# Dense projections of two mixers: float32 products of 64 stationary columns, in pairs, for three float32r products of split operands

## The chip, the core and the metric

The kernel runs on one core of one Trainium2 chip. The metric is the device time of one execution, in microseconds (us), as the median of three runs. The engines are named as in the profile: PE (TensorE's matmuls), PEld (its weight loads), DVE (VectorE), ACT (ScalarE), POOL (GpSimd), SP (the queue that issues most DMAs). The two operands of a matmul are called stationary (loaded into the array, up to 128 columns of it) and moving (streamed through, here 256 or 512 columns).

## What is computed

Two layers of a decoder trunk on 512 tokens of 1024 features, in float32. Each layer is a mixer and a mixture of experts, with a residual sum and a layer norm after each. Cut to what the change touches:

```python
# layer 0: RWKV-7 (8 heads x 64) and causal pooling (windows 2, 4, 8, 16)
p = x @ w_in                               # 1024 -> 2304 features
y_rwkv = ...                               # delta-rule state, head norm, bonus, gate
y_pool = ...                               # pooled groups times pool_w
y = concatenate([y_rwkv, y_pool]) @ w_out  # 1024 -> 1024
x = layer_norm(ALPHA * x + y); x = layer_norm(ALPHA * x + moe(x))
# layer 1: a convolution module (512 channels, width 31) and retention (8 heads x 64)
p = x @ w_in                               # 1024 -> 3072 features
c = silu(norm(depthwise_conv(glu(p[..., :1024]))))
r = group_norm(retention(q, k, v)) * silu(g)
y = concatenate([c, r]) @ w_out
x = layer_norm(ALPHA * x + y); x = layer_norm(ALPHA * x + moe(x))
```

The products with `w_in` and `w_out` are what is called dense below.

## The kernel before

The four parts run one after the other: mixer 0 (to about 336 us of the profiled span), the mixture of layer 0 (to about 512), mixer 1 (to about 836), the mixture of layer 1.

A mixer is written as streams, Python generators that each emit one line of work: `dense` (the projections), `evacuate` (reads each bank of results out of PSUM), `weights` (prepares weights), in mixer 0 `prep`, `solve`, `side`, `states`, `heads` and `pools`, in mixer 1 `turn`, `join`, `kernels`, `taps`, `conv_norm`, `retention`, `ret_norm`. The class `Flow` puts their steps into one order when the program is built: it keeps an expected time for every engine and tile, gives each instruction an expected cost (`cost`, `clocked`), and always takes the stream, by priority, whose next step can start. The chip then runs every engine's instructions in exactly that order. All of them are issued through one helper, so they share line L57 in the profile and are told apart by tile names.

**A dense product** is one step of `unit`: 128 rows of the contraction times one bank of results. It adds into a PSUM tile `pp` of 128 partitions by 512 or 256 columns. In mixer 0 there are 208 products with 512 moving columns (18 column blocks of `w_in` by 8, and 64 of the output projection). In mixer 1 there are 192 with 256 columns (six jobs `qkv`), 96 with 512 (two `conv` pairs and two `gr` jobs), and 64 with 512 of the output projection. `jobs` lists them in the order of use.

**Precision by splitting.** A float32 operand is kept as two float32r tiles: a rounded copy, made on ACT, and the rest, a subtraction on DVE or POOL. Of weights these are `wh` and `wl` (from the fetched `wr`). x^T lives in four tiles `x` of `x_room`, two high and two low, each for half of the features; what goes into the output projections is split likewise (`yT` and `pT` in mixer 0, `mc` and `mr` in mixer 1). A dense product is then three matmuls of 128 stationary columns: high by high, high by low, low by high. `weights` splits a job's weights two jobs ahead: in mixer 0 the subtraction runs on DVE, in mixer 1 on POOL, but for two halves.

**Mixer 0.** `solve` inverts, for each of four pairs of heads, a triangular matrix by repeated squaring: small products `pi` of 64x64 on PE, an addition into `T` and a transposition `Tt` on DVE, level after level. `dense` steps are put into the gaps.

**Mixer 1.** `taps` does the depthwise convolution on DVE: 4 channel groups by 31 taps, each one instruction `acc<-u,cw,acc` over 128x512. Its input `u` comes from the `conv` jobs. When all taps are done, `conv_norm` normalises over channels, tile by tile, which takes PE transposes of `acc` and back of `cn`; only then can the first half of the output projection run.

After its last reader is gone, the room of x^T is given to other tiles: the stream that loads the first expert weights (`start`) waits for the mark `room`.

Of the kernel before, what the change touches and what calls it, by code (L numbers as in the profile page):

```python
# [14 lines left out]
OP = mybir.AluOpType  # L15
# [15 lines left out]
class Flow:  # L31
    """Puts the work of several streams into one order. A stream is a generator that yields, before each step, the engine
    the step starts on and the tiles it needs; the order follows from when those are expected to be there, with
    `streams` in order of priority."""
# [28 lines left out]
    def cost(e, op, out, ins, alu=None):  # L63
# [91 lines left out]
    def take(self, pool, shape, name, bufs):  # L155
        """a tile of a ring, once the reads of the one before it there have been put in order"""
# [13 lines left out]
    def run(self, streams):  # L170
# [79 lines left out]
class Kernel:  # L250
# [12 lines left out]
    def setup(self):  # L263
# [12 lines left out]
        # x^T of a mixer; after its projections what the mixture of experts starts with  # L276
# [3 lines left out]
    def x_room(self, order=(0, 1, 2, 3)):  # L280
# [10 lines left out]
    def mixer0(self):  # L291
        """Feature-major tiles hold two heads on the partitions and 512 tokens; token-major ones hold two chunks of 64 tokens
        (p = 0, 1) on the partitions, and 4 pairs of chunks, heads and features along them. With L the part of a chunk's
        own tokens, T = (I - L)^-1, W = T a and u0 = T (a k^T v), the state after a chunk is
        decay (S + b^T (W S + u0) + k^T v), so all but the product with S is made for every chunk at once."""
# [6 lines left out]
        with ctx:  # L302
# [19 lines left out]
            # weights in the order of their use  # L322
            # (numbers: columns of the input projection; else rows of the output projection: whose, which, a half of the columns)
# [3 lines left out]
            items = []  # L327
            for job in jobs:
# [5 lines left out]
            raws, halved = {}, {}  # L334
# [7 lines left out]
            def halve(raw, eng, e):  # L342
                """the float32r part of weights, and the rest"""
                hi = wp.tile(list(raw.shape), F32R, name="wh")
                lo = wp.tile(list(raw.shape), F32R, name="wl")
                nk, n = raw.shape[1:]
                cuts = [(slice(0, nk // 2), slice(0, n)), (slice(nk // 2, nk), slice(0, n))] if nk > 1 else [
                    (slice(0, 1), slice(0, n // 2)), (slice(0, 1), slice(n // 2, n))]
                for k, c in cuts:
                    yield "A", (raw,)  # L350
                    A.copy(hi[:, k, c], raw[:, k, c])
                for k, c in cuts:
                    yield e, (hi,)
                    eng.tensor_tensor(lo[:, k, c], raw[:, k, c], hi[:, k, c].bitcast(F32), op=OP.subtract)
                return hi, lo
# [9 lines left out]
            fetch(1)  # L365
            # lnx_g for tokens on partitions
# [22 lines left out]
            for t in range(NT):  # L389
                for g in range(2):  # L390
# [4 lines left out]
                    hi, lo = [xT[j][g][:, :, 128 * t:128 * t + 128] for j in range(2)]  # L395
                    A.copy(hi, ps)
                    V.tensor_tensor(lo, ps, hi.bitcast(F32), op=OP.subtract)
# [6 lines left out]
            yT = [[sp.tile([128, S], F32R, name=f"yT{k}{j}") for k in range(2)] for j in range(2)]  # L404
            yp = sp.tile([128, 4, S], F32, name="yp")
            pT = []
# [5 lines left out]
            def weights():  # L412
                for n in range(len(items)):
                    if n >= 2:
                        yield from wait(("wdone", n - 2))
                    halved[n] = yield from halve(raws.pop(n), V, "V")
                    done.add(("w", n))
                    fetch(n + 2)

            units = []  # L420

            def unit(parts):
                """one bank's worth of products: parts [(left, right)] for every 128 rows"""
# [4 lines left out]
                for k, (lhs, rhs) in enumerate(parts):  # L428
                    yield "PE", (lhs[0], lhs[1], rhs[0], rhs[1])
# [3 lines left out]
                    for i, j in ((0, 0), (0, 1), (1, 0)):  # L433
                        mm(ps, lhs[i], rhs[j], start=k == 0 and i + j == 0, stop=k == len(parts) - 1 and i == 1)
# [5 lines left out]
            def dense():  # L440
                """the input projection and the output projection"""
                for n, job in enumerate(jobs):
                    if not isinstance(job, int):
                        yield from wait(*((job[0], k) for k in job[1]))
                    yield from wait(("w", n))
                    wt = halved.pop(n)
                    if isinstance(job, int):
                        yield from unit([([w[:, k, :] for w in wt], [x[k // 4][:, k % 4, :] for x in xT]) for k in range(KT)])
                        if job == last_in:
                            done.add("x^T")  # L450
                    else:
                        left = pT if job[0] == "p" else yT
                        for t, h in tokens(job[2]):
                            ts = slice(128 * t, 128 * t + 128)
                            c = slice(0, 512) if job[2] is not None else slice(512 * h, 512 * h + 512)
                            yield from unit([([q[:, k, ts] if left is pT else q[k][:, ts] for q in left],
                                              [w[:, i, c] for w in wt]) for i, k in enumerate(job[1])])
                        if job == ("p", (2, 3), 1):
                            done.add("room")
                    done.add(("wdone", n))  # L460
# [1735 lines left out]
```

## Time and profile before

| | us |
|---|---|
| median of three runs | 1039.68 |
| their range | 1038.59 to 1040.19 |
| span of the profiled execution | 1034.8 |
| busy in it: PE | 914.6 |
| DVE | 734.7 |
| ACT | 339.5 |
| POOL | 327.5 |

The profile shows one execution, so the sums below stand against its span; the median of the runs lies 4.9 us above it. The page lists the busy time of each engine over the whole span. For a change in two of four parts that share says little: a view that splits the span at the borders of its stages shows which engine is full in which. Matmuls are pipelined, so the printed duration of one overlaps the next; what a matmul costs is read from start to start.

### The profile page before, as it was taken

To read this page: it belongs to the slowest core of one execution; us is meant where nothing else is said; L and a number is where in the kernel's file an instruction comes from. 1 tells how busy PE (TensorE), PEld (TensorE's weight loads), DVE (VectorE), ACT (ScalarE), POOL (GpSimd) and SP (SyncE) were. 2 spreads that over 40 slices of the span, in tenths; PEclk is the share of its full clock that TensorE was granted. 3 is DMA by queue.
4 is the path that set the end of the run, shared out by engine and by line. 5 is a ranking of instruction groups with operands and counts; after the bars stand their busy time and mean duration, and the time that the engine had idled before them with its cause. 6 is when DMAs were issued, how large, how long until landed. Compare 5 with 4: busy or idle time off the path is not lost. (4 is left out here: it accounts for less than half of the span.)

```text
span 1034.8 us, 18665 instructions
## 1 busy us (share of the span) xinstructions
PE 914.6 (88%) x7364; PEld 644.3 (62%) x7364; DVE 734.7 (71%) x1527; ACT 339.5 (33%) x690; POOL 327.5 (32%) x298
## 2 busy tenths in 40 slices
PE   6999999999995599999879589779999748999993
PEld 5777777777775255545368568778878624545542
DVE  3565868576777977776676999994733698767666
ACT  3543242433214233433353012212502333433333
POOL 2120414135303810100169446663422281100003
PEclk9999999999997799999989789988888969999997
DMA  7210101011176859788152121221325165976742
GB/s 216 82 43 22 43 24 41 24 43 60 43 280 221 307 225 359 274 345 334 42 161 76 47 81 42 82 82 41 116 102 214 62 246 227 347 282 247 306 197 83
DMA packets 60012, 156.97 MB, mean 152 GB/s; under 512 B 5153, under 2 KB 40097, under 8 KB 51728
## 3 DMA queue, kind: packets, MB, share of 16 engines
q1 hardware_dynamic: 54256, 141.79, 37.4%
q0 software_dynamic: 4512, 9.74, 3.0%
q10 hardware_dynamic: 1152, 4.19, 1.0%
q8 instruction: 60, 0.98, 0.4%
q14 instruction: 32, 0.26, 0.1%
HBM read 155.71 MB, written 6.29 MB: 157 GB/s over the span
## 5 line engine op out<-in xcount | busy, mean ns | idle before, releaser
L1874 DVE SCALAR_TENSOR_TENSOR x<-x,pcm 128x512 f32<-128x512 f32 x210 | 137.0, 683 | 54.5 <-PE pcm L1872 54.2
L57 PE MATMUL pp<-x,wh 128*128 128x512 f32 x480 | 163.5, 423 | 6.4 <-DVE u L57 5.1
L57 PE MATMUL pp<-wh,x 128*128 128x256 f32 (+1 forms) x544 | 139.2, 342 | 23.3 <-DVE u L57 11.4
L57 DVE SCALAR_TENSOR_TENSOR acc<-u,cw,acc 128x512 f32<-128x512 f32 x120 | 127.8, 1120 | 0.7
L57 ACT CAST wh<-wr 128x512 fp32r<-128x512 f32 (+1 forms) x82 | 61.8, 776 | 192.5 <-PE pp L57 129.0
L57 PEld LDWEIGHTS pp<-wh,x 128*128 128x128 f32 x544 | 100.2, 209 | 34.6 <-DVE u L57 11.6
L1835 PE MATMUL ph<-we,xt 128*64 128x256 f32 (+1 forms) x928 | 116.8, 389 | 0.0
L57 PEld LDWEIGHTS pp<-x,wh 128*128 128x128 f32 x480 | 85.9, 195 | 29.0 <-issue 6.2
L1872 PE MATMUL pcm<-yh,P 128*128 128x512 f32 x216 | 99.2, 459 | 3.0 <-DVEq L2043 2.3
L57 PE MATMUL pp<-x,wl 128*128 128x512 f32 x240 | 96.3, 401 | 0.0
L57 POOL TENSOR_TENSOR wl<-wr,wh 128x1024 fp32r<-128x1024 f32 x28 | 83.3, 2988 | 34.5 <-ACT wh L57 34.5
L57 PE MATMUL pp<-wl,x 128*128 128x256 f32 (+1 forms) x272 | 91.1, 335 | 0.0
L1872 PE MATMUL pcm<-yl,P 128*128 128x512 f32 x216 | 85.8, 397 | 5.1 <-DVE yl L288 5.1
L1824 ACT ACTIVATE xt<-pt,x 128x128 f32<-128x128 f32 x224 | 84.8, 471 | 15.6 <-PE pt L1818 15.6
L1835 PEld LDWEIGHTS ph<-we,xt 128*64 128x64 f32 (+1 forms) x928 | 56.8, 129 | 47.1 <-issue 31.7
L1738 POOL DMA_INDIRECT xg<-xd,imx x20 | 19.9, 993 | 191.9 <-PE pt L1818 147.3
L1872 PEld LDWEIGHTS pcm<-yh,P 128*128 128x128 f32 x216 | 40.6, 188 | 52.0 <-DVE x L1874 28.7
L57 DVE SCALAR_TENSOR_TENSOR x<-x,pp 128x512 f32<-128x512 f32 x64 | 43.6, 685 | 39.6 <-PE pp L57 39.5
L1857 PE MATMUL py<-we,hT 128*64 128x512 f32 (+1 forms) x232 | 62.8, 628 | 0.4 <-ACT hT L1847 0.4
L288 DVE TENSOR_TENSOR yl<-py,yh 128x512 fp32r<-128x512 f32 x54 | 37.1, 691 | 34.3 <-ACT yh L287 34.3
L1839 ACT ACTIVATE hs<-ph 128x128 f32<-128x128 f32 x28 | 7.8, 277 | 160.0 <-PE ph L1835 160.0
L57 PEld LDWEIGHTS pp<-wl,x 128*128 128x128 f32 x272 | 57.4, 211 | 2.8
(427 smaller groups left out, 1657.7 us busy)
## 6 DMA issues: line engine op xcount, KB each, us to landing
we<-in_c_experts_dram SPq DMA_DIRECT2D x56, 1536.0 KB, 9.5
wr<-in_ev_w_in_dram SPq DMA_DIRECT2D x18, 512.0 KB, 3.9
x<-in_c_experts_dram SPq DMA_DIRECT2D x8, 1024.0 KB, 6.1
wr<-in_od_w_in_dram SPq DMA_DIRECT2D x7, 1024.0 KB, 5.1
wr<-in_ev_w_out_dram SPq DMA_DIRECT2D x8, 512.0 KB, 3.7
x<-in_c_experts_dram SPq DMA_DIRECT2D x8, 512.0 KB, 4.2
xd<-x ACTq DMA_DIRECT2D x8, 512.0 KB, 4.1
wr<-in_od_w_in_dram SPq DMA_DIRECT2D x8, 512.0 KB, 5.7
```

The lines of the kernel that those rows point to most:

```text
L57: r = f(*args, **kw)
L288: (eng or nc.vector).tensor_tensor(lo, src, hi.bitcast(F32), op=OP.subtract)
L1738: G.indirect_dma_start(out=xg[n % NG], out_offset=None, in_=xd, in_offset=bass.IndirectOffsetOnAxis(ap=idx, axis=0), bounds_check=S - 1, o ...
L1824: A.activation(xt[:, kk], ps[:, k], AF.Identity, scale=gc[:, kk:kk + 1], bias=bc[:, kk:kk + 1])
L1835: mm(hp[r], xt[:, k, r], w[0][:, k], start=k == 0, stop=k == KT - 1)
L1839: A.activation(hs, hp[:, 0], AF.Silu)
L1857: mm(ps[r], hT[:, r], w[1][:, h], start=True, stop=True)
L1872: mm(ps, P[:, 128 * t:128 * t + 128], y[:, 512 * half:512 * half + 512], start=n == 0, stop=n == len(ops) - 1)
L1874: V.scalar_tensor_tensor(xs, xs, scale, ps, op0=OP.mult, op1=OP.add, accum_out=total)
```

## The change

Operands are no longer split. Weights go from the fetched tile `wr` straight into the matmuls, x^T is two float32 tiles, and `yT`, `yp`, `acc` and `mr` are single float32 tiles. A dense product becomes a pair of float32 matmuls, one for the first 64 stationary columns, with the results on partitions 0 to 63, and one for the other 64, on partitions 64 to 127 (`paired`). The stream `weights` is gone; `wr` has a ring of five (mixer 0) or four tiles (mixer 1), fetched that far ahead. `Flow.cost` gets an entry for such a matmul, n/2380 us for n columns, so 0.215 us for 512 and 0.43 us for a pair of them. The mark `room` comes at the end of the input projection of either mixer (before: after the pooling half, or the convolution half, of the output projection).

```diff
@@ Flow.cost
                 narrow = ins[0].shape[0] <= 64 and out.shape[0] <= 64
+                if out.shape[0] <= 64 and not narrow:
+                    return max(n / 2380, 0.055)
                 return max(0.027 + n / 1200, 0.08) if narrow else max(n / 600, 0.137)
@@ Flow.clocked
-        passes = 1 if op == "transpose" or lhs.dtype != F32 else 2
+        passes = 1 if op == "transpose" or lhs.dtype != F32 or out.shape[0] <= 64 < lhs.shape[0] else 2
@@
-        t = [self.xp.tile([128, 4, S], F32R, name=f"x{n}") for n in order]
-        return t[:2], t[2:]
+        return [self.xp.tile([128, 4, S], F32, name=f"x{n}") for n in order]
+    @staticmethod
+    def paired(mm, out, lhsT, rhs, **kw):
+        for c in (slice(0, 64), slice(64, 128)):
+            mm(out[c], lhsT[:, c], rhs, **kw)
@@ mixer0
+            depth = 5
...
-                    raws[n] = wp.tile([128, nk, m], F32, name="wr")
+                    raws[n] = wp.tile([128, nk, m], F32, name="wr", bufs=depth)
...
-                    A.copy(hi, ps)
-                    V.tensor_tensor(lo, ps, hi.bitcast(F32), op=OP.subtract)
+                    (V.tensor_copy if g else A.copy)(xT[g][:, :, 128 * t:128 * t + 128], ps)
@@ mixer0 unit
-                    yield "PE", (lhs[0], lhs[1], rhs[0], rhs[1])
+                    yield "PE", (lhs, rhs)
...
-                    for i, j in ((0, 0), (0, 1), (1, 0)):
-                        mm(ps, lhs[i], rhs[j], start=k == 0 and i + j == 0, stop=k == len(parts) - 1 and i == 1)
+                    self.paired(mm, ps, lhs, rhs, start=k == 0, stop=k == len(parts) - 1)
@@ mixer0 dense
-                    yield from wait(("w", n))
-                    wt = halved.pop(n)
+                    wt = raws.pop(n)
...
                         if job == last_in:
-                            done.add("x^T")
+                            done.add("room")
...
+                    fetch(n + depth)
@@ mixer0 heads
-                    V.scalar_tensor_tensor(yg, ps.rearrange("p c t -> p (c t)"), lb[:, i:i + 1], gv, op0=OP.add, op1=OP.mult)
+                    V.scalar_tensor_tensor(yT[i], ps.rearrange("p c t -> p (c t)"), lb[:, i:i + 1], gv, op0=OP.add, op1=OP.mult)
...
-                    A.copy(yT[0][i], yg)
-                    e = "V" if i == 3 else "G"
-                    yield e, (yT[0][i],)
-                    (V if i == 3 else G).tensor_tensor(yT[1][i], yg, yT[0][i].bitcast(F32), op=OP.subtract)
@@ mixer1
+            for n in range(1, depth + 1):
+                fetch(n)
...
-            xT = self.x_room((3, 1, 2, 0))
+            xT = self.x_room((3, 1))
@@ mixer1 weights
-                        (V if e == "V" else G).tensor_tensor(lo[:, k], raw[:, k], hi[:, k].bitcast(F32), op=OP.subtract)
@@ mixer1 turn
-                aff, hi, lo = ("AAV", "VAG", "AAV", "VAG")[g]
+                aff = "AVAV"[g]
...
-                (A.copy if hi == "A" else G.tensor_copy)(d, xf)
-                yield lo, (xT[0][g // 2],)
-                (G if lo == "G" else V).tensor_tensor(e, xf, d.bitcast(F32), op=OP.subtract)
@@ mixer1 dense
-                            yield from unit([([m[:, k, ts] for m in mc], [w[:, k, :] for w in wt]) for k in range(4)])
-                        if i:
-                            done.add("room")
+                            yield from unit([(acc[k][:, ts], wt[:, k, :]) for k in range(4)])
...
                     if n == 11:
-                        done.add("x^T")
+                        done.add("room")
@@ mixer1 conv_norm
-                    A.copy(mc[0][:, i], acc[i])
-                    e = "V" if flow.free["V"] < flow.free["G"] + 0.6 else "G"
-                    yield e, (mc[0],)
-                    (V if e == "V" else G).tensor_tensor(mc[1][:, i], acc[i], mc[0][:, i].bitcast(F32), op=OP.subtract)
@@ mixer1 ret_norm
-                    V.tensor_tensor(mr[n][1], yr, mr[n][0].bitcast(F32), op=OP.subtract)
+                    mr[n] = lp.tile([128, 4, 128], F32, name="mr")
+                    V.tensor_tensor(mr[n], yr, sgr[0][:, :, ts], op=OP.mult)
```

Since `Flow` makes the order from its costs, the rest of the program is put in another order too. Three places show it.

PE, the first dense products of mixer 0. `pp` is a bank of results, `x` a tile of x^T, `pm` a small product of `prep`; 64x512 is the shape of the result. Before:

```order
L57 MATMUL pp<-x_140,wh 128x512
L57 MATMUL pp<-x_142,wh 128x512
L57 MATMUL pp<-x_140,wl 128x512
L57 MATMUL pp<-x_140,wh 128x512
L57 MATMUL pp<-x_142,wh 128x512
```

After:

```order
L57 MATMUL pp<-x_146,wr 64x512 x8
L57 MATMUL pp<-x_147,wr 64x512 x8
L57 MATMUL pp<-x_146,wr 64x512 x8
L57 MATMUL pp<-x_147,wr 64x512 x6
L57 MATMUL pm<-z_234,wa_128 128x512
L57 MATMUL pp<-x_147,wr 64x512 x2
L57 MATMUL pp<-x_146,wr 64x512 x4
```

Three matmuls for each 128 rows became two, and none of them waits for `wh` or `wl`.

PE, the inversion for the last pair of heads in mixer 0. `T`, `nf`, `X` and `Tt` are the small matrices of the levels, `py` a product of `states`. Before:

```order
L57 MATMUL pi<-T_2602,nf_2608 64x64 x8
L57 MATMUL pi<-T_2621,nf_2627 64x64 x8
L57 MATMUL py<-Sa,R 64x64 x4
L57 MATMUL pi<-X_2713,Tt_2601 64x64 x8
L57 MATMUL pp<-x_141,wh 128x512
L57 MATMUL pp<-x_143,wh 128x512
L57 MATMUL pp<-x_141,wl 128x512
L57 MATMUL pi<-X_2732,Tt_2620 64x64 x8
```

After:

```order
L57 MATMUL pi<-T_2634,nf_2636 64x64 x8
L57 MATMUL pi<-T_2651,nf_2653 64x64 x8
L57 MATMUL pi<-X_2668,Tt_2633 64x64 x8
L57 MATMUL pi<-X_2681,Tt_2650 64x64 x8
L57 MATMUL pi<-T_2634,nf_2640 64x64 x8
L57 MATMUL pi<-T_2651,nf_2657 64x64 x8
L57 MATMUL pi<-X_2716,Tt_2633 64x64 x8
L57 MATMUL pi<-X_2729,Tt_2650 64x64 x8
```

The dense products between the levels are gone: when this inversion starts, all but 16 of the 208 have been issued (before: 116 of them).

PE, the normalisation after the taps in mixer 1. `acc` are the taps' sums, `cn` the normalised tile. Before:

```order
L57 MATMUL pt<-ident,acc_6036 128x128
L57 MATMUL pt<-ident,acc_6037 128x128
L57 MATMUL pt<-ident,acc_6038 128x128
L57 MATMUL pt<-ident,acc_6039 128x128
L57 MATMUL pp<-wh,x_6033 128x256
L57 MATMUL pp<-wl,x_6033 128x256
L57 MATMUL pp<-wh,x_6035 128x256
L57 MATMUL pr_7428<-qkv_6040,sc 128x64 x4
```

After:

```order
L57 MATMUL pr_7038<-R,qx 128x64
L57 MATMUL pt<-ident,acc_5645 128x128
L57 MATMUL pt<-ident,acc_5646 128x128
L57 MATMUL pt<-ident,acc_5647 128x128
L57 MATMUL pt<-ident,acc_5648 128x128
L57 MATMUL pt<-ident,cn 128x128 x4
L57 MATMUL pt<-ident,acc_5645 128x128
```

Before, the last job of the input projection and the retention lie between the four tiles' transposes; now these four follow each other with nothing between, and the whole output projection comes behind them.

## Rows read from the trace of the kernel before

**Rows 1.** Stages: us from:to, length, busy us per engine, PE's granted clock, DMA share.

```profile
core 0: us, PE busy (x) PEld busy (x) DVE busy (x) ACT busy (x) POOL busy (x), PEclk, DMA share, GB/s
17.00:205.00 188.00, 186.69 (x2424) 137.20 (x2424) 120.73 (x301) 76.00 (x131) 42.40 (x50) 1.00 0.15 44
205.00:283.00 78.00, 76.63 (x919) 57.23 (x919) 57.09 (x149) 21.68 (x42) 31.26 (x40) 1.00 0.16 49
...
556.00:697.00 141.00, 109.55 (x664) 99.55 (x663) 140.28 (x177) 24.87 (x32) 85.51 (x50) 0.88 0.22 69
697.00:743.00 46.00, 45.81 (x294) 39.16 (x295) 24.59 (x73) 17.60 (x37) 18.10 (x13) 0.83 0.17 58
743.00:820.00 77.00, 74.78 (x368) 62.10 (x366) 33.73 (x97) 18.95 (x31) 17.89 (x16) 0.87 0.36 138
```

**Rows 2.** Timeline, PE: dense in mixer 0 (start, us, engine, line, operation, count).

```profile
43.55 0.61 PE L57 MATMUL pp<-x,wh 128*128 128x512 f32 x2
...
44.23 0.61 PE L57 MATMUL pp<-x,wh 128*128 128x512 f32 x2
```

**Rows 3.** Timeline, PE: dense of 256 columns in mixer 1.

```profile
649.82 0.28 PE L57 MATMUL pp<-wl,x 128*128 128x256 f32 x1
...
650.18 0.28 PE L57 MATMUL pp<-wl,x 128*128 128x256 f32 x1
```

**Rows 4.** Timeline, PE: float32 pairs of 64 stationary columns in the mixture.

```profile
340.10 0.38 PE L1835 MATMUL ph<-x,xt 128*64 128x256 f32 x1
340.10 0.38 PE L1835 MATMUL ph<-we,xt 128*64 128x256 f32 x1
...
340.53 0.38 PE L1835 MATMUL ph<-x,xt 128*64 128x256 f32 x1
```

**Rows 5.** Timeline, PE: a float32 pair of 512 columns between float32r products.

```profile
438.21 1.08 PE L1857 MATMUL py<-we,hT 128*64 128x512 f32 x4
439.22 0.50 PE L1872 MATMUL pcm<-yh,P 128*128 128x512 f32 x1
```

**Rows 6.** Timeline, PE: four float32 products of 128 stationary columns.

```profile
895.80 1.89 PE L1835 MATMUL ph<-x,xt 128*128 128x256 f32 x8
897.35 0.58 PE L1872 MATMUL pcm<-yh,P 128*128 128x512 f32 x1
```

**Rows 7.** Timeline, PE: a dense product among products of the inversion.

```profile
221.25 0.73 PE L57 MATMUL pp<-x,wh 128*128 128x512 f32 x2
...
222.14 0.68 PE L57 MATMUL pi<-X,Tt 64*64 64x64 f32 x16
```

**Rows 8.** Timeline, DVE: one turn of the inversion, with DVE's idle time.

```profile
222.87 0.42 DVE L57 TENSOR_TENSOR T<-T,pi 128x256 f32<-128x256 f32 x1 [0.60 <-PE pi L57]
223.32 0.45 DVE L57 STREAM_TRANSPOSE Tt<-T 128x256 f32<-128x256 f32 x1
```

**Rows 9.** Page, costliest groups: the taps, and POOL's subtractions (busy us, mean ns).

```profile
L57 DVE SCALAR_TENSOR_TENSOR acc<-u,cw,acc 128x512 f32<-128x512 f32 x120 | 127.8, 1120 | 0.7
...
L57 POOL TENSOR_TENSOR wl<-wr,wh 128x1024 fp32r<-128x1024 f32 x28 | 83.3, 2988 | 34.5 <-ACT wh L57 34.5
```

**Rows 10.** Timeline, DVE then POOL: three taps before and three beside a subtraction.

```profile
636.48 2.29 DVE L57 SCALAR_TENSOR_TENSOR acc<-u,cw,acc 128x512 f32<-128x512 f32 x3
...
639.94 6.56 DVE L57 SCALAR_TENSOR_TENSOR acc<-u,cw,acc 128x512 f32<-128x512 f32 x3
640.29 5.65 POOL L57 TENSOR_TENSOR wl<-wr,wh 128x1024 fp32r<-128x1024 f32 x2
```

**Rows 11.** Timeline, PE: first dense of mixer 1, the taps' end, the output projection.

```profile
528.71 0.39 PE L57 MATMUL pp<-wh,x 128*128 128x256 f32 x1
...
696.97 0.69 PE L57 MATMUL pt<-ident,acc 128*128 128x128 f32 x2 [6.26 <-DVE acc L57]
...
743.25 0.78 PE L57 MATMUL pp<-wh,x 128*128 128x512 f32 x1
...
818.78 0.39 PE L57 MATMUL pp<-wh,mr 128*128 128x512 f32 x1
```

More of the change, by code (lines that the diff above doesn't have):

```diff
@@ L364, in mixer0 @@
             w0, a0, kk, ka, rk, lb, psc = (vec[:, 14 + 4 * i:18 + 4 * i] for i in range(7))
-            fetch(1)
+            for n in range(1, depth):
+                fetch(n)
             lg = sp.tile([128, 4, 128], F32, name="lg")
@@ L444, in dense @@
                         yield from wait(*((job[0], k) for k in job[1]))
-                    yield from wait(("w", n))
-                    wt = halved.pop(n)
+                    wt = raws.pop(n)
                     if isinstance(job, int):
-                        yield from unit([([w[:, k, :] for w in wt], [x[k // 4][:, k % 4, :] for x in xT]) for k in range(KT)])
+                        yield from unit([(wt[:, k, :], xT[k // 4][:, k % 4, :]) for k in range(KT)])
                         if job == last_in:
-                            done.add("x^T")
+                            done.add("room")
                     else:
-                        left = pT if job[0] == "p" else yT
                         for t, h in tokens(job[2]):
@@ L918, in pools @@
                     flow.give(room)
-                    done.add(("pooled", g))
-                yield from wait("x^T")
-                pT.extend(self.xp.tile([128, 4, S], F32R, name=f"x{j}") for j in (1, 2))
-                for g in range(4):
-                    yield "A", (yp,)
-                    A.copy(pT[0][:, g], yp[:, g])
-                    yield "G", (pT[0],)
-                    G.tensor_tensor(pT[1][:, g], yp[:, g], pT[0][:, g].bitcast(F32), op=OP.subtract)
-                    done.add(("p", g))
+                    done.update((("pooled", g), ("p", g)))
             def room(pool, name):
@@ L934, in mixer0 @@
             begin = self.start(0, flow, np_, room(pi, "pi"), room(pm, "pm"))
-            flow.run([solve(), evacuate(), *begin, states(), pools(), prep(), heads(), side(), weights(), dense()])
+            flow.run([solve(), evacuate(), *begin, states(), pools(), prep(), heads(), side(), dense()])
     def mixer1(self):
@@ L1000, in mixer1 @@
             total = {}
-            mc, mr, us, rn, units, sgr = [], {}, {}, {}, [], []
+            mr, us, rn, units, sgr = {}, {}, {}, [], []
             done, wait = flow.done, flow.wait
             bank = lambda pool, shape, name: flow.take(pool, [128] + shape, name, 2)
-            def weights(first=0, last=len(jobs)):
-                for n in range(first, last):
-                    if n >= 2:
-                        yield from wait(("wdone", n - 2))
-                    elif n:
-                        yield from wait(("xT", 1))
-                    raw = raws.pop(n)
-                    hi = wp.tile(list(raw.shape), F32R, name="wh")
-                    lo = wp.tile(list(raw.shape), F32R, name="wl")
-                    cuts = [slice(0, raw.shape[1] // 2), slice(raw.shape[1] // 2, raw.shape[1])]
-                    for k in cuts:
-                        yield "A", (raw,)
-                        A.copy(hi[:, k], raw[:, k])
-                    for i, k in enumerate(cuts):
-                        e = "V" if 0 < n < 3 and i else "G"
-                        yield e, (hi,)
-                        (V if e == "V" else G).tensor_tensor(lo[:, k], raw[:, k], hi[:, k].bitcast(F32), op=OP.subtract)
-                    halved[n] = hi, lo
-                    done.add(("w", n))
-                    fetch(n + 2)
             def sums():
@@ L1131, in unit @@
                         units.append(ps)
-                    for p, q in ((0, 0), (0, 1), (1, 0)):
-                        mm(ps, lhs[p], rhs[q], start=k == 0 and p + q == 0, stop=k == len(parts) - 1 and p == 1)
+                    self.paired(mm, ps, lhs, rhs, start=k == 0, stop=k == len(parts) - 1)
                 done.add(("unit", k0))
@@ L1138, in dense @@
                 for n, (what, i) in enumerate(jobs):
-                    yield from wait(("w", n))
-                    wt = halved.pop(n)
+                    wt = raws.pop(n)
                     if what == "qkv":
@@ L1144, in dense @@
                             ts = slice(128 * t, 128 * t + 128)
-                            yield from unit([([q[k // 4][:, k % 4, ts] for q in xT], [w[:, k, :] for w in wt]) for k in range(KT)], 256)
+                            yield from unit([(xT[k // 4][:, k % 4, ts], wt[:, k, :]) for k in range(KT)], 256)
                     elif what in ("conv", "gr"):
@@ L1148, in dense @@
                         for j in range(2):
-                            yield from unit([([w[:, k, 128 * j:128 * j + 128] for w in wt], [q[k // 4][:, k % 4, :] for q in xT])
-                                             for k in range(KT)])
+                            yield from unit([(wt[:, k, 128 * j:128 * j + 128], xT[k // 4][:, k % 4, :]) for k in range(KT)])
                     elif what == "oc":
@@ L1261, in conv_norm @@
                     flow.give(room)
-                yield from wait("x^T")
-                mc.extend(self.xp.tile([128, 4, S], F32R, name=f"x{j}") for j in range(2))
-                for i in range(4):
-                    yield "A", (acc[i],)
-                    A.copy(mc[0][:, i], acc[i])
-                    e = "V" if flow.free["V"] < flow.free["G"] + 0.6 else "G"
-                    yield e, (mc[0],)
-                    (V if e == "V" else G).tensor_tensor(mc[1][:, i], acc[i], mc[0][:, i].bitcast(F32), op=OP.subtract)
                 done.add("mc")
@@ L1399, in mixer1 @@
             begin = self.start(1, flow, lp, room(pt, "pt"), room(ps_, "ps"))
-            flow.run([weights(0, 1), sums(), turned(), *begin, *(join(t) for t in range(NT)), ret_norm(), retention(), kernels(), evacuate(), conv_norm(), taps((0, 2)), taps((1, 3)), weights(1), dense(), affine(), *(turn(h, g) for h in range(2) for g in range(4))])
+            flow.run([sums(), turned(), *begin, *(join(t) for t in range(NT)), ret_norm(), retention(), kernels(), evacuate(), conv_norm(), taps((0, 2)), taps((1, 3)), dense(), affine(), *(turn(h, g) for h in range(2) for g in range(4))])
     def moments(self, pool, x):
```

68 lines of the change are left out of this document (15 added, 53 removed).

## The prediction

> **What bounds the kernel now.** I read the page first: PE is busy for 914.6 of 1034.8 us, more than any other engine. That is an average over four parts, and the change is in two of them, so I split the span at the borders of the stages [rows 1]. From 17 to 283 us, in mixer 0, PE is busy for 186.69 of 188 us and then for 76.63 of 78. DVE has 121 and 57 us of work there. Whatever is added to PE here is added to the time, and whatever DVE, ACT or POOL lose is hidden by PE. In mixer 1, from 556 to 697, it is the other way: DVE has 140.28 of 141 us and PE 109.55. After that PE is full again (45.81 of 46, 74.78 of 77).
>
> Next I read what a dense product costs, from start to start, since the printed durations overlap. In mixer 0 three float32r matmuls take 0.68 us (43.55 to 44.23) [rows 2]. With 256 columns in mixer 1 three take 0.36 (649.82 to 650.18) [rows 3].
>
> **The price of the new product.** The mixtures already run the new form. Two float32 matmuls of 64 stationary columns and 256 moving ones start together, one record each; such a matmul has two records (16 matmuls of the program's order are 32 records here), so that a pair is two such steps, 340.10 to 340.53, or 0.43 us [rows 4]. With 512 columns a pair, four records, takes 438.21 to 439.22, 1.01 us, with entry and exit [rows 5]; twice 0.43 is 0.86, so 0.15 is left for those. Four plain float32 products of 128 stationary columns and 256 moving ones take 895.80 to 897.35, or 0.39 each [rows 6]: the halves side by side win nothing over a whole. I take 0.86 us for 512 columns (before: 0.68) and 0.43 for 256 (before: 0.36). The pair thus has fewer matmuls and costs a quarter more.
>
> The Trainium skill (FP8 and Floating Point Precision, section TensorE Precision Notes) says that true float32 goes through the array in four passes. If a pass cost as much as a float32r matmul of rows 2, a product would take 0.91 us in place of 0.86 and mixer 0 some 10 us more than below; the rows show the lower price, and the sum goes by them.
>
> **Mixer 0, the dense term.** 208 products times (0.86 - 0.68) is +37.4 us, all in the stretch where PE is full.
>
> **Mixer 0, changes of form.** A dense product between two products of the inversion takes 221.25 to 222.14, 0.89 us, so 0.21 for leaving and entering the form [rows 7]; for float32 pairs it is 0.15 [rows 5]. In the order dense stands in about 208 separate places before and 188 after. Nothing in the trace shows a float32 pair beside 64x64 tiles. I take no change; at 0.15 it would be -11 us, and I keep +11 for the other side.
>
> **Mixer 0, what the splits did.** ACT's copies and DVE's subtractions go. PE was full while they ran, so they are worth nothing. If that cover were gone, DVE's 121 us in 188 would still be no bound.
>
> **Mixer 0, the last inversion.** The planner expects 0.43 us for a pair and packs two where the chip has time for one. So it has issued 192 of the 208 products when the inversion of the last pair of heads begins, where before 116 had been. That stretch becomes a bare chain between PE and DVE. DVE adds (0.42), transposes (0.45) and then waits for PE (0.60) [rows 8]; PE in turn has nothing during DVE's 0.87. Two matrices go at once, which hides half: 0.45 for each of about 20 turns is 9 us of new idle time on PE. If other streams fill it, 0; if nothing overlaps, 17. I take +9.
>
> Mixer 0 in all: +46 us (26 to 65 at the ends).
>
> **Mixer 1, what DVE gains.** A tap takes 0.76 us when POOL is not subtracting (three in 2.29) and 2.19 beside a subtraction (three in 6.56, POOL's beginning 0.35 us later) [rows 10]. The mean of all 120 is 1.120 us, 127.8 in all, and POOL's 28 subtractions of weights take 83.3 us [rows 9]. Without these the taps need 120 times 0.76, 92 us: DVE's bound from 556 to 697 falls by 36 us. Alone that would be a large gain.
>
> **Mixer 1, what is late next.** It is PE. A job of the input projection is 32 pairs of 0.43 or 16 of 0.86, 13.8 us either way, and there are twelve: 165 us from 528.71 [rows 11], to 694. The second half of x^T now stands on DVE behind eight rotations that wait for the first products; while they do, PE has no further input. I take 4 us for this (0, or 7, which is 16 pairs, half a job). The last input of the rotations is the tenth job: 529 + 4 + 138 = 671. In the order some 54 taps stand on DVE behind these rotations, 41 us, and the retention's work, 25 us by DVE's 24.59 from 697 to 743 [rows 1]. The taps end at 671 + 66 = 737; before it was 697 [rows 11].
>
> Then `conv_norm` stands bare on PE, four tiles of two rounds of four transposes, 1.4 us a round by the 0.69 of two [rows 11]: 11 us, with the chain between them I take 12 (0 if tiles overlap fully, 20). In the kernel before, the last job and the retention covered this. The output projection starts at 749, where before it started at 743.25 [rows 11]. Before, it took 75.5 us, of which 64 products of 0.68 are 43.5 and 32 are other work, part of it the retention, which now comes earlier. After: 64 times 0.86 is 55, with 25 of other work (10 to 32). That ends at 829, against 819 before: +10 us. With all at their low ends it is -20; with all at the high ends, and PE's clock still at 0.87 there [rows 1], +28.
>
> **Elsewhere.** The first weights no longer wait for a copy, and expert weights can be fetched earlier. The mixtures' own work is as it was. I take 0 for this.
>
> **The sum.** 46 + 10 is +56 us on 1034.8, a span of 1091. The median of the runs is 4.9 us above the profiled span: 1096.
>
> **Rivals.**
> (A) The pair is as cheap as the planner has it, 0.43 us for 512 columns. Both halves stream the same moving operand here, while in rows 4 and 5 two different ones go side by side; that is the one thing for it. Then mixer 0 loses 208 times 0.25, 52 us, of which I keep 40 since the inversions' chain becomes the bound; in mixer 1 the taps end 36 us earlier and the output projection is 64 times 0.25, 16 us, shorter: about 1040 - 92 = 948. Against it: the whole 128 columns of rows 6 cost what the pair costs. The side is decided by the price of the pair. Mixer 0 gives 208 (p - 0.68) + 9, mixer 1 gives 10 - 224 (0.86 - p), since 160 products lie ahead of the last rotations and 64 behind the taps; the sum is nothing at p = 0.73. Chance 0.05. The Trainium skill (TensorEngine Tiling (Array Packing), section Theoretical Speedup) gives up to twice the speed where a dimension is at most 64, which would be this case; rows 4 to 6 do not show it for halves of a 128-column product.
> (B) The new order does no harm: mixer 0 costs the 37 of its dense term and mixer 1, with DVE freed, ends 10 us earlier. 1040 + 27 = 1067. For it: the planner can move other streams into the gaps. Against it: the orders above show bare stretches. Chance 0.20.
> (C) The planner's wrong price costs more: engines wait in order for a PE that is late everywhere, mixer 0 at +60 and mixer 1 at +30: 1130. Chance 0.15.
> (D) The two halves do not run together, since they read one moving operand: 1.72 us a product. Over the forecast that is 0.86 for each of the 208 products of mixer 0 and of the 224 on mixer 1's path, 372 us: 1468. Rows 4 speak against it, where two start at once. Chance 0.03.
> The forecast itself has 0.57.
>
> **Range and chances.** A and D lie outside any useful range. From 1064 to 1134 the range holds the forecast with the bounds of its terms, most of B and most of C. About 0.2% can be told from no change here. Slower by more than that: forecast, C, D and nearly all of B, 0.93; within it 0.02 (the low end of B); faster 0.05 (A).
>
> **What the profile after should show.** Dense pairs of 512 columns 0.86 us apart in mixer 0 and PE over 95% busy until the last inversion; then a stretch in which PE idles on `T` and `Tt` of DVE. The mixture of layer 0 begins some 46 us later. In mixer 1 the taps at a median and mean of about 0.76, DVE no longer full, PE full from 529 (shifted) for 165 us, the taps' end 40 us later within the mixer, the transposes of `acc` with PE idle about them. The forecast is wrong if a pair takes 0.73 or less, if PE in mixer 0 has no more work than before, or if the mixer-1 taps end earlier than the 168 us after its first dense product that they needed before.

## The result, and the profile after

The changed kernel takes 1168.2 us (1167.95 to 1169.23), against 1039.68 before: the ratio is 1.124, interval 1.122 to 1.126. The profiled execution spans 1166.1 us, 131.3 more than that of before. The forecast was slower, 1096; the direction was right, and the time lies 34 us above the range.

The page of the changed kernel, engines first, then PE in 40 slices of the span and the clock granted to it:

```profile
PE 1027.8 (88%) x7924; PEld 546.2 (47%) x7924; DVE 636.3 (55%) x1457; ACT 265.6 (23%) x578; POOL 218.2 (19%) x256
...
PE   6999999899787747999977999999859966999994
...
PEclk9999999879978868999987999998558986999997
```

PE is busy 113 us longer and DVE 98 us less. But digits between the 8th and the 16th slice (mixer 0) and around the 29th and 30th (the end of mixer 1) are not full, and the clock is low in the same places. Before, mixer 0 had 99% and then 98% of PE busy at full clock [rows 1].

Reading the same events in both traces puts the 131.3 us in place: mixer 0, to the first matmul of the first experts, 337.2 before and 426.7 after: +89.5. The mixture of layer 0: +2.1. From there to mixer 1's first dense product: 16.9 and 21.9, +5.0. Mixer 1 from its first dense product to its last, 290.1 [rows 11] and 322.0: +31.9. The rest: +2.8.

Stages of the changed kernel in mixer 0, columns as in [rows 1]:

```profile
core 0: us, PE busy (x) PEld busy (x) DVE busy (x) ACT busy (x) POOL busy (x), PEclk, DMA share, GB/s
17.00:180.00 163.00, 161.06 (x1580) 71.65 (x1581) 61.57 (x164) 36.90 (x62) 23.84 (x32) 1.00 0.22 66
180.00:326.00 146.00, 133.34 (x1244) 66.84 (x1246) 59.47 (x145) 26.11 (x42) 26.92 (x39) 0.89 0.09 29
326.00:400.00 74.00, 55.60 (x870) 38.01 (x862) 41.60 (x129) 8.03 (x18) 13.33 (x15) 0.86 0.11 42
```

Until 180 us PE is as full as before. From there it rests 31 us in 220, while DVE, ACT and POOL are each busy for less than six tenths of the time: the chain of the inversions passes from one to another, and nothing fills PE.

The price of a pair is the one that was forecast. Timeline of PE in mixer 1, 128 records of 512 columns, which are 32 pairs, and the start of what follows:

```profile
643.94 27.64 PE L57 MATMUL pp<-x,wr 128*64 128x512 f32 x128
671.40 0.82 PE L57 MATMUL pp<-wr,x 128*64 128x256 f32 x6
```

From start to start that is 27.46 / 32, or 0.858 us a pair. To see what else PE's time went to, I summed the steps from each matmul's start to the next one's in mixer 0, apart by kind and by the clock granted at the start (us; the runs in the last two columns come below):

```
                        before   changed   right price   before, dense early
dense                    166.9     198.1       199.6           153.2
other, full clock        143.1     133.7       149.7           110.7
other, half clock          3.6      41.7         3.6            84.4
PE idle                   18.5      48.3        16.9            76.8
```

Dense costs 31 us more. By the price alone, 208 products at 0.858 for 0.68, it would be 37; what the runs of dense take above their price fell from 25 to 20 us. The other 58 us are idle time (+30) and small products at half clock (+38, against 9 less at full clock).

### The profile page after: what moved, and what is told of

Its sections match the earlier page's. It is cut to its first block, busy times and chain, and to the rows that moved or that the text cites. A ratio compares the mean times of both kernels' runs of the same rounds, so it can differ in the third digit from the quotient of the medians.

```text
span 1166.1 us, 19502 instructions
## 1 busy us (share of the span) xinstructions
PE 1027.8 (88%) x7924; PEld 546.2 (47%) x7924; DVE 636.3 (55%) x1457; ACT 265.6 (23%) x578; POOL 218.2 (19%) x256
## 5 line engine op out<-in xcount | busy, mean ns | idle before, releaser
L57 PE MATMUL pp<-x,wr 128*64 128x512 f32 x960 | 224.3, 606 | 1.1 <-DVE x L57 0.7
L57 PEld LDWEIGHTS pp<-x,wr 128*64 128x64 f32 x960 | 64.1, 138 | 110.5 <-issue 104.2
L57 DVE SCALAR_TENSOR_TENSOR acc<-u,cw,acc 128x512 f32<-128x512 f32 x120 | 86.5, 768 | 0.6
L57 PE MATMUL pp<-wr,x 128*64 128x256 f32 x640 | 70.6, 380 | 0.0
L57 PEld LDWEIGHTS pp<-wr,x 128*64 128x64 f32 x640 | 45.6, 137 | 24.1 <-issue 2.0
L1791 PEld LDWEIGHTS pcm<-yl,P 128*128 128x128 f32 x216 | 42.1, 195 | 9.7 <-DVE yl L296 6.4
L1737 PE MATMUL pt<-ident,xg 128*128 128x128 f32 x224 | 37.9, 296 | 9.1 <-DMA xg<-xd,ixh 9.1
L57 ACT COPY X<-pi 128x256 f32<-128x256 f32 x40 | 14.9, 372 | 129.5 <-PE pi L57 129.1
L57 DVE TENSOR_TENSOR T<-T,pi 128x256 f32<-128x256 f32 x32 | 13.2, 413 | 51.9 <-PE pi L57 51.9
L57 POOL TENSOR_TENSOR qkv<-qkv,rot 128x128 f32<-128x128 f32 x32 | 19.1, 616 | 109.0 <-DVE rot L57 109.0
```

The lines of the kernel that those rows point to most:

```text
L57: r = f(*args, **kw)
L1737: nc.tensor.transpose(ps[:, k], xrows[:, 128 * kk:128 * kk + 128], self.ident)
L1791: mm(ps, P[:, 128 * t:128 * t + 128], y[:, 512 * half:512 * half + 512], start=n == 0, stop=n == len(ops) - 1)
```

## The experiments

**The price in the planner alone.** The change tells the planner 0.43 us for a pair that takes 0.86. This run corrects that entry, counts the columns as for other float32 matmuls, and adds one mark which the new order needs:

```diff
-                    return max(n / 2380, 0.055)
+                    return max(n / 1190, 0.11)
...
-        passes = 1 if op == "transpose" or lhs.dtype != F32 or out.shape[0] <= 64 < lhs.shape[0] else 2
+        passes = 1 if op == "transpose" or lhs.dtype != F32 else 2
...
+                    if i:
+                        yield from wait(("y", i - 1))
                     M = d["M"] = rp.tile([128, 4, 2, 64], F32, name="M")
```

> The changed kernel with the planner's entry for a float32 matmul of 64 stationary columns at n/1190 us, so that a pair of 512 columns counts 0.86 us as the trace has it (the change: 0.43), its columns counted for the clock as those of other float32 matmuls, and one more planner's mark so that the next inversion takes its tiles only when the states of the pair before have been read. Dense products issued before the four inversions: 36, 67, 92, 116 (changed kernel 38, 70, 144, 192; before 37, 68, 93, 116). Theory 1, the planner's wrong price makes the order that costs what the price of the products does not explain: mixer 0 ends 35 to 45 us later than before in place of 90, mixer 1 takes 0 to 15 us more than before, the whole is 1075 to 1100 us. Rival 1, the float32 pairs themselves cost it (changes of form, a lower clock): within 15 us of the changed kernel, 1150 to 1175.

It took 1088.3 us, ratio 1.045 (1.042 to 1.048). The instructions that compute are those of the changed kernel; the order alone gives back 80 us of the 131. Price and count of columns were changed together, so the run shows what a right account of a pair is worth, not which of the two it takes. Stages of mixer 0 in its trace:

```profile
17.00:173.00 156.00, 155.25 (x1782) 74.67 (x1782) 69.92 (x191) 42.83 (x70) 26.10 (x33) 1.00 0.20 60
173.00:320.00 147.00, 146.63 (x1778) 73.59 (x1778) 77.87 (x218) 27.38 (x50) 39.71 (x51) 1.00 0.17 57
320.00:375.00 55.00, 43.20 (x260) 20.68 (x256) 37.47 (x116) 12.56 (x20) 10.93 (x20) 0.87 0.36 142
```

PE is full at full clock until 320, and mixer 0 ends at 375.0, 37.8 us later than before. That is the dense term of the forecast, 37.4, and no more; the table above shows idle time and half clock back where they were before. Theory 1 stands and rival 1 falls.

Two timelines of PE show what the order does to an inversion. First the last inversion in the changed kernel (start, us, operation, count, idle time before):

```profile
332.42 0.91 PE L57 MATMUL pi<-T,nf 64*64 64x64 f32 x16 [2.17 <-DVE T L57]
333.88 1.12 PE L57 MATMUL pi<-T,nf 64*64 64x64 f32 x16 [0.55 <-DVE T L57]
334.75 1.74 PE L57 MATMUL pi<-X,Tt 64*64 64x64 f32 x32
336.45 1.47 PE L57 MATMUL pi<-T,nf 64*64 64x64 f32 x32
```

Then the same place with the right price:

```profile
235.23 0.68 PE L57 MATMUL pi<-T,nf 64*64 64x64 f32 x16 [0.27 <-DVE T L57]
235.84 1.08 PE L57 MATMUL pp<-x,wr 128*64 128x512 f32 x4
236.85 0.68 PE L57 MATMUL pi<-T,nf 64*64 64x64 f32 x16
237.37 0.63 PE L57 MATMUL pi<-X,Tt 64*64 64x64 f32 x16
```

In the second a dense pair lies between the levels, and 16 small products take 0.68. In the first PE waits for `T`, then runs 16 in 0.91 and 1.12: it works at half clock, after it has rested. In these traces the clock halves in stretches in which PE rests, or just behind them; what exactly makes it fall was not tried.

**One matmul of 128 columns for each pair, in the order of the change.**

```diff
-        for c in (slice(0, 64), slice(64, 128)):
-            mm(out[c], lhsT[:, c], rhs, **kw)
+        mm(out, lhsT, rhs, **kw)
...
+                if out.tensor.name.startswith("pp"):
+                    return max(n / 1190, 0.11)
...
-        passes = 1 if op == "transpose" or lhs.dtype != F32 or out.shape[0] <= 64 < lhs.shape[0] else 2
+        passes = 1 if op == "transpose" or lhs.dtype != F32 else 2
...
+                    if i:
+                        yield from wait(("y", i - 1))
```

> The changed kernel with one float32 matmul of 128 stationary columns for each pair, counted by the planner as a pair of the change (0.43 us for 512 columns), so that the order stays nearly the same. Theory 1 with the price read from the mixtures: a whole costs what a pair costs, 0.86 us, and the time is within 1% of the changed kernel, 1157 to 1180. Rival 2, halves side by side are what is dear (entering and leaving the form of 64 columns some 94 times in mixer 0): 10 to 25 us faster than the changed kernel. Rival 3, halves side by side do win something: 30 us slower or more.

1166.3 us, ratio 1.119 (1.115 to 1.123), within 0.2% of the changed kernel. Its timeline: 30 records of 512 columns (15 matmuls) and 64 of 256 (32 matmuls):

```profile
665.71 13.04 PE L57 MATMUL pp<-x,wr 128*128 128x512 f32 x30
678.58 13.98 PE L57 MATMUL pp<-wr,x 128*128 128x256 f32 x64
692.39 7.89 PE L57 MATMUL pp<-x,wr 128*128 128x512 f32 x18
```

From start to start that is 0.858 and 0.432 us: a whole costs what the pair costs (0.858), as [rows 4, 6] said. Rivals 2 and 3 fall: neither are the halves dear to enter, nor does putting them side by side win anything. The equal totals hide two differences, mixer 0 being 8.6 us longer here and mixer 1 6.4 shorter; the order is not quite the same, and the run doesn't say what makes them. This run also has the mark of the first one, and so shows that the mark is not what helped there.

**The kernel before, with its own matmuls priced at half.**

```diff
-            return n / 2330
+            return n / 4660
```

> The kernel before with the planner's price of its float32r matmuls halved (n/4660 in place of n/2330), the same instructions in another order: dense products before the four inversions 40, 72, 102, 141 (before 37, 68, 93, 116). Theory 1: slower than before by 25 to 70 us, with dense ahead of the inversions and the chain of the last one bare. Rival 1, the order matters little: within 10 us of 1040.

1066.6 us, ratio 1.023 (1.020 to 1.027), at the lower end of what was expected. Mixer 0 is 10.7 us longer and mixer 1 13.9. The same instructions in a worse order cost time without any float32 pair, but less than in the changed kernel; here 141 products lie ahead of the last inversion, there 192.

**The kernel before, with dense as early as in the change.**

```diff
-            return n / 2330
+            return n / 1900
...
+                    if i:
+                        yield from wait(("y", i - 1))
```

The mark of the first run is here too, which the kernel before doesn't have.

> The kernel before with its float32r matmuls priced at n/1900 (before: n/2330). By that the planner thinks the array never reaches its full clock and puts dense ahead wherever PE looks idle: 88, 112, 144 and 192 products before the four inversions, the last two as in the changed kernel (144, 192), the first two not (38, 70). The instructions are those of before. Theory 1, an inversion without dense products between its levels leaves PE idle and lowers its clock: mixer 0 takes 25 to 50 us more than before, PE's idle time in it 35 to 60 us in place of 18, other work at half clock 20 us or more in place of 4; 1065 to 1100 in all. Rival 1, the bare chain costs little: mixer 0 within 10 us of before.

1189.3 us, ratio 1.145 (1.142 to 1.148): 89 us above the upper end. Mixer 0 alone is 93 us longer (430.1 for 337.2), more than in the changed kernel. Its stages:

```profile
17.00:200.00 183.00, 162.99 (x1542) 131.31 (x1544) 81.92 (x185) 58.89 (x103) 23.54 (x33) 0.91 0.19 56
200.00:300.00 100.00, 84.98 (x855) 64.27 (x852) 61.95 (x152) 26.13 (x46) 31.79 (x37) 0.79 0.10 31
300.00:430.00 130.00, 92.40 (x1215) 75.63 (x1213) 74.49 (x241) 29.83 (x50) 28.89 (x38) 0.78 0.24 91
```

PE rests in every stage, and the clock is 0.78 to 0.91 (last column of the table above: 77 us idle, 84 at half clock). So an order that spends the dense work early can take more than 90 us of mixer 0, with the fast products of before. How much of it the mark adds was not tried; with the right price it did mixer 0 no harm. I had expected half, since I counted only the last inversion; the stretches before it lose their filling too. Its mixer 1 is 57 us longer as well, by 47 us of idle PE; why this order harms mixer 1 so much was not followed further.

**Mixer 1 alone, with the right price.** Mixer 0 is that of before, with its four tiles of x^T. In mixer 1 the edit against the changed kernel is the price, and with it the count of columns as in the first run:

```diff
-                    return max(n / 2380, 0.055)
+                    return max(n / 1190, 0.11)
```

> Mixer 0 of the kernel before, mixer 1 of the changed kernel with the right price for a pair (as in the run with the price alone). Theory 1: the taps lose their slow ones, mean 0.77 us in place of 1.12, PE is the bound of the input projection at 13.8 us a job, and mixer 1 takes -10 to +15 us against before: 1030 to 1055. Rival 4, the new bound on PE costs mixer 1 what it cost in the changed kernel, 37 us with the start of it: 1070 to 1080.

1056.0 us, ratio 1.012 (1.006 to 1.017), just above the upper end. In the profiled execution, which took 1060.4 (the fastest took 1050.6), mixer 1 proper is 13.8 us longer than before, and mixer 1's first dense product comes 6.9 us later after the mixture's start. Rival 4 falls: with a right price mixer 1 keeps some of what DVE gains, and yet it does not win.

**Mixer 1 of before without the rest of the weights.** This shows what DVE gains if PE's work stays as it is; the results then lack that part of the weights.

```diff
-                        (V if e == "V" else G).tensor_tensor(lo[:, k], raw[:, k], hi[:, k].bitcast(F32), op=OP.subtract)
+                    if n < 12:
+                        lo = hi
```

> The kernel before, but mixer 1's input projection leaves out the subtraction that makes the rest of the weights: POOL's and DVE's subtractions of twelve jobs are gone, and the matmuls that would take the rest take the rounded weights again, so PE does the same work. Theory 1, POOL's subtractions slow the taps beside them: the taps' mean falls from 1.12 to 0.74 to 0.80 us, they end some 36 us earlier, PE's idle time in mixer 1 falls from 35 us to under 12, and the whole is 1004 to 1020. Rival 5, the slow taps come from other traffic: mean over 1.0 us and 1035 to 1042.

1008.4 us, ratio 0.971 (0.969 to 0.973). Mixer 1 proper is 37.1 us shorter (253.0), and its first dense product comes 8.5 us later. The taps by the view of tile `acc` on DVE (count, ns min/median/max, first and last start). The kernel before:

```profile
L57 DVE SCALAR_TENSOR_TENSOR acc<-u,cw,acc x120: 736/742/2894, 557.1 to 696.2; 128x512 f32<-128x512 f32 x120
```

This run:

```profile
L57 DVE SCALAR_TENSOR_TENSOR acc<-u,cw,acc x120: 734/740/2695, 563.5 to 664.5; 128x512 f32<-128x512 f32 x120
```

The changed kernel:

```profile
L57 DVE SCALAR_TENSOR_TENSOR acc<-u,cw,acc x120: 732/746/1527, 659.3 to 855.1; 128x512 f32<-128x512 f32 x120
```

The changed kernel with the right price:

```profile
L57 DVE SCALAR_TENSOR_TENSOR acc<-u,cw,acc x120: 737/752/943, 605.6 to 703.0; 128x512 f32<-128x512 f32 x120
```

POOL's subtractions were what slowed the taps (rival 5 falls): without them their mean is 0.787 us for 1.120, they span 101 us, before 139, and the kernel gains 31 us. The trace of before says the same tap by tap: 57 taps with nothing of POOL beside them took 0.74 us on average (0.75 at most), 43 beside a subtraction of weights 1.60 (the other 20 lie beside other work of POOL). One such tap, and the subtraction:

```profile
640.81 2.88 DVE L57 SCALAR_TENSOR_TENSOR acc<-u,cw,acc 128x512 f32<-128x512 f32 x1
640.29 2.85 POOL L57 TENSOR_TENSOR wl<-wr,wh 128x1024 fp32r<-128x1024 f32 x1
```

The three taps of [rows 10] took 0.95, 2.88 and 2.88, so their mean of 2.19 is no even slowing: each of the last two ended only after the subtraction beside it. With the right price the float32 kernel has that gain too, 97 us; in the order of the change the taps last 196. A tap reads two tiles, `u` and `acc`. The Trainium skill (GPSIMD Engine Reference, section Specifications) says that POOL shares its ways into SBUF with DVE and is in contention with instructions that have two inputs there; these traces agree (1.60 us for 0.74).

**Half of the rows in float32, in mixer 1's input projection.** If POOL's subtractions slow DVE and float32 slows PE, a mixture should lie below both kernels. Mixer 0 and the output projections are those of before; of each product's eight blocks of rows the first four are one float32 matmul (0.86 us in the planner), the others stay split.

The main lines of a longer edit:

```diff
-                    hi = wp.tile(list(raw.shape), F32R, name="wh")
+                    hi = wp.tile([128, 4, 512 if n >= 12 else 256], F32R, name="wh")
...
-yield from unit([([q[k // 4][:, k % 4, ts] for q in xT], [w[:, k, :] for w in wt]) for k in range(KT)], 256)
+yield from unit([(xA[:, k, ts], wraw[:, k, :]) for k in range(4)] + [([q[:, k, ts] for q in xT], [w[:, k, :] for w in wt]) for k in range(4)], 256)
```

> Mixer 0 as before. In mixer 1's input projection the first four of eight 128-row blocks of every job are one float32 matmul of 128 stationary columns (priced 0.86 us for 512 columns), the other four stay three float32r matmuls of split operands; POOL splits half as many weights. The output projection as before. Theory 1: PE gets 15 us more (half of the jobs' 96 products of 512 and 192 of 256 at 0.18 and 0.07 more), DVE loses 18 us of slow taps, PE's idle 35 us takes the difference: mixer 1 10 to 20 us shorter than before, 1018 to 1032 in all. Rival 6, PE becomes the bound as in the changed kernel: 1038 to 1055.

1036.2 us against 1039.1 for before on the same chip, ratio 0.997 (0.994 to 0.999): faster than before by 0.3%, and short of the 1018 to 1032 that were expected; rival 6 doesn't describe it either. The stage that holds its taps:

```profile
566.00:678.00 112.00, 95.67 (x439) 72.72 (x437) 111.04 (x162) 14.05 (x18) 48.04 (x31) 0.97 0.21 66
```

The taps are done in 112 us, before 139, and DVE is still the bound there. Mixer 1 from its first dense product to its last is 4.3 us shorter (285.8), but that first product comes 5.7 us later after the mixture's start, in the profiled execution (1041.1 us).

## Why the prediction was wrong, step by step

**The price of a pair and the dense term: right.** 0.86 was forecast and 0.858 measured. With the order repaired, mixer 0 is 37.8 us longer, for 37.4.

**Changes of form: right at nothing.** Dense stands in 104 runs before and 94 after, which are the 208 and 188 changes that the text counted, and with the right price the runs of dense take 4 us less above their price than before (21 for 25), while the steps that lead into them take 5 us more (21 for 16). The bound of 11 us was too wide: it set the 0.21, which is for leaving and entering together, against each change.

**The last inversion: the step that failed.** I put the planner's wrong price at 9 us (0 to 17), counting the turns of one inversion, in them only the idle time that DVE's work leaves on PE, and nothing for PE's clock. It costs mixer 0 51.7 us, the changed kernel's 426.7 less the right price's 375.0. By the table 31 of them are idle time of PE, and 22 are the clock: 38 us more of small products at half clock, for only 16 less at full clock (dense differs by 1.5). Stages of the changed kernel around its last two inversions, which start at 236.6 and 325.5, columns as in [rows 1]:

```profile
200.00:250.00 50.00, 43.29 (x345) 23.55 (x336) 22.84 (x72) 8.96 (x14) 16.99 (x25) 0.80 0.12 39
250.00:297.00 47.00, 47.00 (x424) 18.75 (x424) 19.88 (x36) 2.98 (x8) 2.92 (x4) 1.00 0.11 35
297.00:325.50 28.50, 22.54 (x278) 15.41 (x274) 12.51 (x25) 9.82 (x14) 3.94 (x5) 0.83 0.01 1
325.50:366.00 40.50, 32.12 (x679) 27.51 (x679) 20.60 (x73) 7.13 (x16) 6.85 (x9) 0.87 0.01 2
366.00:400.00 34.00, 23.98 (x192) 10.98 (x192) 21.17 (x59) 0.90 (x2) 6.47 (x6) 0.85 0.23 89
```

The second of them again, with PE's dense matmuls alone (162 records, four to a product):

```profile
250.00:297.00 47.00, 38.20 (x162) 1.00 0.11 35
```

The idle time that I priced lies in the fourth row, which has 8.4 us of it in all, so 9 was not too small for that. What I left out are the first, third and fifth row, with 23 us more of idle time, and the clock, 0.80 to 0.87 in all four. No dense matmul starts from 220 to 245 us, nor from 301 to 373; with the right price no pause between dense matmuls of mixer 0 is longer than 4.1 us. Between the levels of the third inversion (second row) some 40 dense products still lie, and there PE is full at full clock. So it is not the inversion alone that stands bare, but all the small products before and behind it that dense had covered. The profile of before could have told it: PE was full at full clock [rows 1] because dense lay in every gap [rows 7].

**Mixer 1: the mechanism right, its size a third.** I had +10 us and it was +31.9. The taps did lose their slow ones (mean 0.768 us for 1.120, [rows 9]), and PE was late instead. But I forecast 300 us from the first dense product to the last, and it took 322: `conv_norm` began 25 us later than forecast and took 8 longer, the output projection was 11 shorter. The taps ended 230 us after the first dense product; I had 208. DVE waited for PE, rotation by rotation, in the changed kernel and much less with the right price. DVE's waits from the first dense product to the last (engine, what waits, for what: us, times, longest), in the changed kernel:

```profile
DVE qkv L57 <- PE pp L57: 46.5, 16, 15.5
...
DVE u L57 <- PE pp L57: 31.4, 4, 12.9
```

And with the right price:

```profile
DVE qkv L57 <- PE pp L57: 18.7, 6, 6.6
...
DVE u L57 <- PE pp L57: 12.9, 1, 12.9
```

The input projection ended at 804 us. From there the last taps share DVE with the retention, whose small products on PE, and then `conv_norm`, have no dense beside them either. Columns as in [rows 1]:

```profile
825.00:855.00 30.00, 24.11 (x113) 19.55 (x111) 22.41 (x56) 1.75 (x3) 2.00 (x1) 0.50 0.00 1
855.00:878.00 23.00, 10.95 (x43) 8.73 (x43) 10.74 (x34) 4.51 (x12) 3.78 (x5) 0.50 0.00 1
```

`conv_norm` stood bare, as forecast, but for 20 us and not 12, at half clock. The forecast named a low clock for the high end of its range only, and its +28 there is reached by the other terms (3, 8 and 7 us above the +10), so the clock was put at nothing here too. PE in the changed kernel:

```profile
858.65 1.11 PE L57 MATMUL pt<-ident,acc 128*128 128x128 f32 x4
863.41 1.11 PE L57 MATMUL pt<-ident,cn 128*128 128x128 f32 x4 [3.65 <-DVE cn L57]
...
873.79 1.06 PE L57 MATMUL pt<-ident,acc 128*128 128x128 f32 x4
877.67 1.09 PE L57 MATMUL pt<-ident,cn 128*128 128x128 f32 x4 [2.82 <-DVE cn L57]
878.68 3.68 PE L57 MATMUL pp<-wr,acc 128*64 128x512 f32 x8
```

The output projection, 69 us, was shorter than the 80 forecast. With the right price the taps end 132 us after the first dense product, while the input projection still runs and covers `conv_norm`; mixer 1 is then 296.1 us, 6.0 more than before: 31 more of dense, set against 29 less of idle PE. So the order costs mixer 1 26 us.

**Elsewhere: nearly right.** 0 was forecast; it is 2.1 in the mixture of layer 0, 5.0 between the mixture and mixer 1's first dense product, and 2.8 at the end.

**The rivals.** (A), the cheap pair, and (D), halves that do not run together, fell with the 0.858. (B), an order that does no harm, at 1067, comes nearest to the run with the right price, and that took 1088: mixer 1 did not end earlier than before. (C), the planner's wrong price, names the cause that the runs show, with 90 and 37 us where it said 60 and 30. Its mechanism, engines that wait for a late PE, is seen in mixer 1; in mixer 0 it is PE that waits. It had 0.15, although the diff and the trace stood in plain contradiction by a factor of two. In place of a small term for one inversion, the contradiction should have been priced from the stretches that it empties.

## What to carry to other kernels

Where an order is made from expected costs, compare each new cost entry with the trace first; if it is off by a factor, the whole order can be off (25 us in one kernel here, 80 in another), and the bill is not the error in the entry but the filling that it takes from dependent chains. Look for every stretch that is left without filling, not only the one that stands out, and price it as two parts: the engine's idle time in it, and its small work at the lower clock. The work that has moved ahead is no third part, as the engine has it to do in either order. And a gain on an engine that was the bound counts only as far as the next engine has room: DVE's gain in mixer 1 is worth 31 us with PE's work unchanged, and nothing with PE's 31 us of dearer products.

## What the runs showed of the hardware

A float32 product of 128 stationary columns took 0.858 us for 512 columns, whole or as two halves side by side. Taps of 0.74 us on DVE became up to 2.9 beside a subtraction on POOL of 2.8. Where PE waited among small products, it was granted half its clock for part of the time: 0.86 on average from 326 to 400 us of the changed kernel, with 18 us of idle time, and 0.78 from 200 to 430 us in the run with dense early, with 53.
